# Two-block network on one core: experts on eight chunks of 64 rows instead of four of 128, high and low parts side by side in one stationary operand

## The chip, the cores and the metric

The kernel runs on one core of one Trainium2 chip, in one launch. The metric is the device time of one execution in microseconds, and the time given is the median over several runs. PE is TensorE (matmul), DVE is VectorE, ACT is ScalarE, POOL is GpSimd; SP is the engine that issues the DMAs here.

## The reference, cut to what matters

The network is two layers of a first block, then one second block, on 256 tokens of width 1024. The change is in the last stage, a mixture of 32 experts. A router takes each token to one of four groups, then to two of the eight experts of this group, and gives two weights; every expert is a gated network of width 256:

```python
g_top, g_idx = lax.top_k(g_prob, 1)
e_top, e_loc = lax.top_k(jax.nn.softmax(e_in, axis=-1), 2)
gate = sum(one_hot(e_glob, 32) * weights)
hdn = silu(xc @ w1[e]) * (xc @ w3[e])
out = sum over e of ((hdn * gate[:, e]) @ w2[e])
```

So there are 512 (token, expert) rows. With the reference's own inputs its router picks 20 of the 32 experts. Their rows, in the order of the experts, are 21, 10, 38, 58, 17, 3, 26, 19, 3, 1, 2, 1, 3, 14, 73, 3, 2, 145, 27, 46.

Laid end to end, these 512 rows fall into chunks. With four chunks of 128 the experts in each are 5, 11, 4 and 3 (an expert that crosses a border counts in both chunks). With eight chunks of 64 they are 3, 3, 4, 8, 4, 1, 2 and 2; an expert that ends exactly on a border is counted in the next chunk too. The sixth small chunk lies wholly inside the expert of 145 rows.

## The kernel before, in words

Matrices are kept as two fp32r parts, a high one (the value rounded) and a low one (the rest). A product takes three matmuls: high by high, high by low, low by high (`mm3`, lines 330 to 335). Each matmul has a 128x128 stationary operand and 512 moving columns in this stage.

The stage is `moe`. Weights lie in HBM as units of 128x1024 fp32 (512 KB). An expert has six: q0 to q3 hold w1 and w3, q4 and q5 hold w2. A unit is fetched by SP (`fetch`, line 1729) into one of six `raw` buffers or one of four `held` buffers, then parted by `parts`: ACT writes the high part (line 1743), DVE subtracts it to get the low part (line 1744). `ahead` holds parts of q0 and q1 of the expert to come, `kept` parts of q4 and q5 of a chunk's last expert.

Rows of the tokens are gathered by expert, 128 to a chunk, with matmuls against a placement matrix `P` (`gather`, lines 1810 to 1822) into `xs`, high and low apart. Which experts a chunk has is known only on the chip: DVE makes the lists `table`, `last` and the counts `items` (lines 1779 to 1829), and the engines read them into registers (lines 1756 and 2008).

The loop over the chunks (lines 1997 to 2018) is, for each chunk:

- SP fetches four units of the chunk's end ahead of time into `held`.
- A nest of `If(n > j + 1)`, one level for each further expert of the chunk (line 2011). Each level that is taken runs one `item` (line 1942): 24 matmuls into `g` (`gu`), 12 matmuls `down` for the expert before it, a `turn` of the hidden rows (two transposes on PE, then a split by ACT and DVE), and the fetch and parting of the next units. A chunk with n experts runs n - 2 items. Where a level isn't taken, every engine jumps to the end of the nest.
- The `edge` (line 1954): the last expert of this chunk and, with the same weights, its rows in the next chunk (`g2`). It parts the four held units, two `kept` and two `ahead`, multiplies for both chunks, does two `down`, and then `finish` (line 1888): DVE scales `y` by `g2`, ACT and DVE split it, and eight matmuls with the transposed placement `PT` add it to the 256 token rows in `acc`.

The first expert (`first`, line 1928) runs beside the gather. PSUM holds `acc` (four banks), `y` (two), and one bank each for `gu` and `tr`. Within an engine the order is that of the scheduler; `issue_after` and `after` bind some instructions behind others, such as the parting of the held units behind the split of the `turn` (lines 1959 and 1960).

Of the kernel before, what the change touches and what calls it, by code (L numbers as in the profile page):

```python
# [224 lines left out]
class K:  # L225
# [1425 lines left out]
    def moe(self, xT, rows, late, h):  # L1651
# [14 lines left out]
        self.fold, ef, lo, one_f, S = cut(72, 36), cut(32, 32), cut(64, 4), cut(128, 32), cut(64, 32)  # L1666
        cut = self.cuts(self.wl_p.tile([128, UNIT], F32R, name="wl"))
        before, ones, er, C, M, C2, act, before2, hot = (
            cut(p, n) for p, n in ((128, 128), (128, 128), (32, 32), (128, 66), (128, 128), (128, 128), (64, 4), (32, 64), (64, 136)))
        C, M, C2 = (a.rearrange("p (t e) -> p t e", t=2) for a in (C, M, C2))  # L1670
        hot = hot.rearrange("p (c j) -> p c j", c=4)
        zeros = mo.tile([128, 128], F32R, name="zeros")
        nc.gpsimd.iota(ef, pattern=[[0, 32]], base=0, channel_multiplier=1, allow_small_or_imprecise_dtypes=True)
        nc.gpsimd.iota(lo, pattern=[[128, 4]], base=-1, channel_multiplier=0, allow_small_or_imprecise_dtypes=True)
# [40 lines left out]
        h = self.t1("h")  # L1715
# [39 lines left out]
        def entry(tile, i):  # L1755
# [5 lines left out]
        st, end, t1, t2, act2 = S[:, 0:1], S[:, 1:2], S[:, 4:8], S[:, 8:12], S[:, 12:16]  # L1761
        nc.vector.tensor_copy(st, pe[:, 2:3])
        nc.vector.tensor_add(end, st, pe[:, :1])
        nc.vector.tensor_scalar(t1, lo, 129.0, end, op0=OP.add, op1=OP.min)
# [4 lines left out]
        self.warm(2, mm(rank[:64, :4], before2, act[:32], start=True, stop=True), *idle)  # L1769
        key = S[:, 16:20]  # L1770
        nc.vector.scalar_tensor_tensor(key, act.bitcast(F32), 64.0, rank[:64, :4], op0=OP.mult, op1=OP.subtract)
        nc.vector.tensor_tensor(out=hot[:, :, :32], in0=key.unsqueeze(2).to_broadcast([64, 4, 32]),
                                in1=self.down[:64, None, :].to_broadcast([64, 4, 32]), op=OP.is_equal)
        pl = self.bank("gu")[:32, :132]
        mm(pl[:, :128].rearrange("p (c j) -> p c j", c=4), er, hot[:32, :, :32], start=True, stop=True)
        self.warm(7, mm(pl[:, 128:], ones[:32, :32], act[:32], start=True, stop=True), *idle)
# [3 lines left out]
        lists, count = pl[:1, :128].rearrange("p (c j) -> p c j", c=4), pl[:1, 128:]  # L1780
        tmp = self.t1("list")
        R, n4 = tmp[:1, :136].rearrange("p (c j) -> p c j", c=4), tmp[:1, 136:140]
        six = self.t1("six")[:1, :128].rearrange("p (c j) -> p c j", c=4)
        nc.vector.tensor_scalar_mul(six, lists, 6.0)
        nc.vector.tensor_copy(items[:, :4], count)
        nc.vector.tensor_reduce(R[:, :, 33], six, axis=AX.X, op=OP.max)
        nc.vector.tensor_copy(n4, count)
        few = lambda a: a.to_broadcast([1, 4, 32])
        nc.vector.tensor_tensor(out=R[:, :, :32], in0=iota[:1, None, :32].to_broadcast([1, 4, 32]),
                                in1=few(n4.unsqueeze(2)), op=OP.is_equal)  # L1790
        nc.vector.tensor_tensor(out=R[:, :, :32], in0=R[:, :, :32], in1=few(R[:, :, 33:]), op=OP.mult)
        nc.vector.tensor_tensor(out=R[:, :, :32], in0=R[:, :, :32], in1=six, op=OP.add)
        table = mo.tile([1, 4, 32], I32, name="table")
# [16 lines left out]
        def gather(xs, s, per, bank):  # L1810

            n = s.stop - s.start
            for k in range(0, 8, per):
                for i in range(2):
                    p = bank()[:, :per * n].rearrange("p (d r) -> p d r", d=per)
                    for d in range(per):
                        for t in range(2):
                            mm(p[:, d], rows[t][i][:, 128 * (k + d):128 * (k + d) + 128], P[:, t, s], start=t == 0, stop=t == 1)
                    if i == 0:
                        yield nc.scalar.activation(xs[i][:, k:k + per], p, AF.Copy)  # L1820
                    else:
                        yield nc.vector.tensor_copy(xs[i][:, k:k + per], p)

        last = mo.tile([1, 8], I32, name="last")
# [4 lines left out]
        nc.vector.tensor_copy(last.rearrange("p (c j) -> p c j", c=4), R[:, :, 32:])  # L1829
        x0, x1 = ([mo.tile([128, 8, 256], F32R, name="xs%d%d" % (n, i)) for i in range(2)] for n in range(2))  # L1830
        chunks = [[x[:, :, 128 * c:128 * c + 128] for x in xs] for xs in (x0, x1) for c in range(2)]
# [4 lines left out]
        gate = mo.tile([128, 136], F32, name="gate")  # L1836
        PT = mo.tile([128, 4, 256], F32R, name="PT")

        def gates():


            self.after(nc.vector.tensor_scalar(t1, lo[:64], 129.0, end, op0=OP.add, op1=OP.is_le), placed)
            nc.vector.tensor_scalar(t2, lo[:64], 128.0, st, op0=OP.add, op1=OP.is_ge)
            nc.vector.tensor_mul(t1, t1, t2)
            nc.vector.tensor_scalar(t2, key, 64.0, None, op0=OP.is_lt)
            nc.vector.tensor_tensor(out=hot[:, :, 32:], in0=t1.unsqueeze(2).to_broadcast([64, 4, 2]),
                                    in1=t2.unsqueeze(2).to_broadcast([64, 4, 2]), op=OP.mult)
# [9 lines left out]
            mine = self.wh_p.tile([128, UNIT], F32R, name="wh")[:64]  # L1857
            nc.vector.tensor_mul(mine[:, :512], mask, pg)
            yield
            pi = self.bank("tr")[:, :136]  # L1860
            for c in range(4):
                mm(pi[:, 34 * c:34 * c + 34], mine[:, 128 * c:128 * c + 128], hot[:, c], start=True, stop=True)
            nc.vector.tensor_copy(gate, pi)
            yield
            for c in range(0, 4, 2):
                p = self.bank("tr")
                self.transposes(p, [P[:, t, 128 * (c + i):128 * (c + i) + 128].bitcast(F32) for i in range(2) for t in range(2)])
# [12 lines left out]

        def down(w, hT, y):
            for half in range(2):
                s = slice(512 * half, 512 * half + 512)
                for k in range(2):
                    ks = slice(128 * k, 128 * k + 128)
                    self.mm3(y[half], (hT[0][:, ks], hT[1][:, ks]), (w[k][0][:, s], w[k][1][:, s]), False, k == 1, True)

        def finish(c, y):

            for half in range(2):  # L1890
                s = slice(512 * half, 512 * half + 512)
                nc.vector.tensor_mul(yg[:, s], y[half], g2[:, s])
                if c < 3:
                    self.split(*(a[:, s] for a in parts_yg), yg[:, s])
            for t in range(2):
                for half in range(2):
                    pt, s = PT[:, c, 128 * t:128 * t + 128], slice(512 * half, 512 * half + 512)
                    if c == 3:
# [5 lines left out]
        def hidden(h, g, c, j):  # L1904
            sg = self.t1("sg")
            nc.scalar.activation(sg, g[:, :256], AF.Silu)
            nc.vector.scalar_tensor_tensor(h, sg, gate[:, 34 * c + j:34 * c + j + 1], g[:, 256:], op0=OP.mult, op1=OP.mult)

        def gu(g, c, w, ds):

            for d in ds:
                s = slice(512 * (d % 2), 512 * (d % 2) + 512)
                i = self.mm3(g, (chunks[c][0][:, d], chunks[c][1][:, d]), (w[d // 2][0][:, s], w[d // 2][1][:, s]),
                             d == 0, d == 7, True)
# [27 lines left out]
        def item(c, j, e, prev, follow, y):  # L1942
# [4 lines left out]
            hT = then(gu(g, c, w, range(4)), h)  # L1947
# [6 lines left out]
        def edge(c, e, follow, y):  # L1954
# [6 lines left out]
            if c < 3:  # L1961
# [7 lines left out]
            h2 = self.t1("h2")  # L1969
# [3 lines left out]
            if c == 3:  # L1973
                down(kept, turn(h2), y)
                finish(3, y)
# [21 lines left out]
        for c in range(4):  # L1997
            y = [ps.tile([128, 512], F32, name="y", tag="y", bufs=2) for _ in range(2)]
            for half in range(2):
                if c:  # L2000
                    nc.vector.memset(y[half], 0.0)
                else:
                    mm(y[half], zeros, x0[0][:, :2].rearrange("p a b -> p (a b)"), start=True, stop=True)
# [12 lines left out]
            if c < 3:  # L2016
# [109 lines left out]
```

## Time and profile before

| what | value |
|---|---|
| median of three runs | 1815.82 us (1813.64 to 1819.9) |
| the profiled execution's own time | 1809.89 us |
| its span, first to last instruction | 1808.1 us |
| mean granted TensorE clock | 0.987 |
| PE, DVE, ACT, POOL busy in the span | 1724.7, 1184.7, 936.7, 62.3 us |
| the expert stage from the first item to the last matmul | 1582.5 to 1797.3 us of the span |

The profile is of one execution; busy times are sums over instructions, and a matmul's end is modelled, so the distance from one matmul's start to the next is the better price. "Idle before" names who ended a wait. Times in views are microseconds from the start of the span.

### The profile page before, as it was taken

What the parts mean: (1) busy time and instruction counts of PE and PEld (TensorE: products, weight loads), DVE (VectorE), ACT (ScalarE), POOL (GpSimd) and SP (SyncE); (2) the same over time, 40 slices, a digit from 0 to 9 for tenths busy, and PEclk for the clock granted to TensorE, in tenths of its full rate; (3) what the DMA queues carried; (4) which work ended last, traced back from release to release, by engine and by line L of the source; (5) the groups of instructions that cost most, each with busy time, mean ns of one, the idle gap of its engine ahead of it and who ended that gap; (6) DMA issues with size and microseconds to landing.
All of it is one profiled execution on the core that took longest, in us unless ns stands there. A gap on an engine that the chain in (4) does not pass through costs nothing. (4 is left out here: it accounts for less than half of the span.)

```text
span 1808.1 us, 26098 instructions
## 1 busy us (share of the span) xinstructions
PE 1724.7 (95%) x9663; PEld 1466.7 (81%) x9663; DVE 1184.7 (66%) x1964; ACT 936.7 (52%) x1454; POOL 62.3 (3%) x85
## 2 busy tenths in 40 slices
PE   9999999999999999999999999999999998799997
PEld 7778899899877887778889899877788796577775
DVE  5675785566666556655687466676566568678776
ACT  5444464654544444444366464654444575467653
POOL 0000002000000000000001100000000001000001
PEclk9999999999999999999999999999999998799999
DMA  8866453234677655865554333558655431489872
GB/s 298 299 221 199 153 174 132 94 112 144 220 232 253 196 198 185 286 214 185 186 177 137 112 106 127 173 198 279 227 191 181 153 128 39 164 316 326 300 252 95
DMA packets 105099, 346.17 MB, mean 191 GB/s; under 512 B 12454, under 2 KB 12710, under 8 KB 104808
## 3 DMA queue, kind: packets, MB, share of 16 engines
q1 hardware_dynamic: 104936, 344.14, 56.1%
q8 instruction: 84, 1.38, 0.3%
q14 instruction: 79, 0.65, 0.1%
HBM read 340.95 MB, written 3.15 MB: 190 GB/s over the span
## 5 line engine op out<-in xcount | busy, mean ns | idle before, releaser
L343 DVE TENSOR_TENSOR wl<-raw,wh 128x1024 fp32r<-128x1024 f32 (+2 forms) x356 | 400.6, 1136 | 180.7 <-ACT wh L343 178.4
L343 ACT ACTIVATE wh<-raw 128x1024 fp32r<-128x1024 f32 (+2 forms) x356 | 346.8, 986 | 304.5 <-PE gu L334 150.3
L333 PE MATMUL gu<-wh,xh 128*128 128x512 f32 (+1 forms) x640 | 255.4, 399 | 4.9 <-ACT xh L343 3.7
L335 PE MATMUL gu<-wh,xl 128*128 128x512 f32 (+1 forms) x640 | 248.3, 388 | 1.7 <-DVE xl L343 1.6
L334 PE MATMUL gu<-wl,xh 128*128 128x512 f32 (+1 forms) x640 | 246.5, 385 | 2.5 <-DVE wl L343 2.5
L333 PE MATMUL gu<-xh,wh 128*128 128x256 f32 x832 | 240.7, 289 | 2.3 <-DVE sp L1209 1.9
L334 PE MATMUL gu<-xl,wh 128*128 128x256 f32 x832 | 236.1, 284 | 0.0
L335 PE MATMUL gu<-xh,wl 128*128 128x256 f32 x832 | 235.9, 284 | 0.0
L333 PEld LDWEIGHTS gu<-xh,wh 128*128 128x128 f32 x832 | 159.5, 192 | 4.4 <-issue 3.2
L334 PEld LDWEIGHTS gu<-xl,wh 128*128 128x128 f32 x832 | 159.4, 192 | 1.1 <-issue 1.0
L335 PEld LDWEIGHTS gu<-xh,wl 128*128 128x128 f32 x832 | 159.3, 192 | 0.0
L335 PEld LDWEIGHTS gu<-wh,xl 128*128 128x128 f32 x640 | 120.2, 188 | 29.4 <-DVE xl L343 5.4
L333 PEld LDWEIGHTS gu<-wh,xh 128*128 128x128 f32 x640 | 120.3, 188 | 27.5 <-ACT xh L343 5.8
L334 PEld LDWEIGHTS gu<-wl,xh 128*128 128x128 f32 x640 | 120.6, 188 | 25.8 <-DVE wl L343 5.0
L343 DVE TENSOR_TENSOR wg<-raw,wg 128x1024 fp32r<-128x1024 f32 x68 | 83.3, 1225 | 74.8 <-ACT wg L343 74.4
L343 ACT ACTIVATE wg<-raw 128x1024 fp32r<-128x1024 f32 x68 | 72.0, 1059 | 99.9 <-DMA raw<-wpk 99.7
L343 DVE TENSOR_TENSOR bl<-raw,bh 128x1024 fp32r<-128x1024 f32 x46 | 56.4, 1225 | 73.2 <-ACT bh L343 73.1
L343 ACT ACTIVATE bh<-raw 128x1024 fp32r<-128x1024 f32 x46 | 48.8, 1061 | 80.5 <-PE acc L335 44.8
L1744 DVE TENSOR_TENSOR wl<-raw,wh 128x1024 fp32r<-128x1024 f32 x72 | 85.5, 1218 | 5.9 <-ACT wh L1743 5.8
L343 ACT ACTIVATE hh<-tr 128x256 fp32r<-128x256 f32 x108 | 40.7, 377 | 91.0 <-PE tr L354 88.7
L1743 ACT ACTIVATE wh<-raw 128x1024 fp32r<-128x1024 f32 x72 | 74.2, 1055 | 9.9 <-DMA raw<-wpk 9.4
L333 PE MATMUL acc<-bh,hh 128*128 128x512 f32 x176 | 70.3, 400 | 9.3 <-ACT hh L343 9.0
(589 smaller groups left out, 3551.9 us busy)
## 6 DMA issues: line engine op xcount, KB each, us to landing
raw<-wpk SPq DMA_DIRECT2D x549, 512.0 KB, 4.2
ada<-wada SPq DMA_DIRECT2D x96, 256.0 KB, 5.0
held<-wpk SPq DMA_DIRECT2D x16, 512.0 KB, 4.9
bc_g<-ln_g SPq DMA_DIRECT2D x8, 512.0 KB, 4.8
bc_b<-ln_b SPq DMA_DIRECT2D x8, 512.0 KB, 6.8
raw<-wpk SPq DMA_DIRECT2D x6, 384.0 KB, 3.4
c<-c SPq DMA_DIRECT2D x8, 256.0 KB, 5.7
kept<-n SPq DMA_DIRECT2D x8, 256.0 KB, 3.3
```

The source lines that it names most:

```text
L333: nc.tensor.matmul(out, ah, bh, start=start, stop=False, skip_group_check=skip)
L334: nc.tensor.matmul(out, ah, bl, start=False, stop=False, skip_group_check=skip)
L335: return nc.tensor.matmul(out, al, bh, start=False, stop=stop, skip_group_check=skip)
L343: return nc.scalar.activation(hi, src, AF.Copy), nc.vector.tensor_sub(lo, src, hi.bitcast(F32))
L1743: hi = nc.scalar.activation(wh, raw, AF.Copy)
L1744: lo = nc.vector.tensor_sub(wl, raw, wh.bitcast(F32))
```

## The change

Rows are cut into eight chunks of 64. A chunk's stationary operand holds the 64 high rows in its left half and the 64 low rows in its right half, so that two matmuls (against the high and the low weights) make all four products, and the two halves of the output partitions are added afterwards. `gu` has 16 matmuls instead of 24 and `down` 8 instead of 12. The sum is made in `turn`: ACT copies both halves of `g` out of PSUM (`hidden`), four small fp32 matmuls with a stacked identity (`both`) transpose and add, then ACT takes the Silu, DVE the product, and ACT and DVE split it into the two halves of `hs`. `finish` puts both halves into `acc` by `PT`, whose rows are doubled (`P2`, `PT`). The lists are of eight chunks. `yg` has a buffer of its own, `PT` takes a buffer that held two `raw` tiles, and `raw` has five tiles instead of six.

The diff, cut to its core:

```diff
-        for _ in range(2):
-            more = self.gt.tile([128, 2, 1024], F32, name="raw", tag="gate")
-            raw_tiles += [more[:, i] for i in range(2)]
-        yg = raw_tiles.pop()
+        more, PT = (self.gt.tile([128, 2, 1024], dt, name="raw", tag="gate") for dt in (F32, F32R))
+        raw_tiles += [more[:, i] for i in range(2)]
+        yg = mo.tile([128, UNIT], F32, name="yg")
...
-        x0, x1 = ([mo.tile([128, 8, 256], F32R, name="xs%d%d" % (n, i)) for i in range(2)] for n in range(2))
-        chunks = [[x[:, :, 128 * c:128 * c + 128] for x in xs] for xs in (x0, x1) for c in range(2)]
+        x0, x1 = (mo.tile([128, 8, 4, 2, 64], F32R, name="xs%d" % n) for n in range(2))
+        chunks = [xs[:, :, c].rearrange("p d i r -> p d (i r)") for xs in (x0, x1) for c in range(4)]
...
+            P2 = self.new_xT()[0].rearrange("p d t -> p (d t)").rearrange("p (t c i r) -> p t c i r", t=2, c=8, i=2)
+            for t in range(2):
+                nc.scalar.activation(P2[:, t], P[:, t].bitcast(F32).rearrange("p (c r) -> p c r", c=8)[:, :, None]
+                                     .to_broadcast([128, 8, 2, 64]), AF.Copy)
...
-            for c in range(0, 4, 2):
+            for c in range(0, 8, 2):
                 p = self.bank("tr")
...
+        def hidden(h, g, c, j):
+
+            a, b = h
+            nc.scalar.activation(a, g[:, :256], AF.Copy)
+            nc.scalar.activation(b, g[:, 256:], AF.Copy, scale=gate[:, 34 * c + j:34 * c + j + 1])
+
         def turn(h, tag="tr"):
-            p = one(tag)
-            self.transposes(p, [h[:, :128], h[:, 128:]])
-            hh, hl = self.t1("hh", F32R), self.t1("hl", F32R)
-            split.append(self.split(hh, hl, p[:, :256]))
-            return hh, hl
+
+            p = one(tag)[:, :256]
+            for k in range(2):
+                for i, a in enumerate(h):
+                    mm(p[:, 128 * i + 64 * k:128 * i + 64 * k + 64], a[:, 128 * k:128 * k + 128], both, start=True, stop=True)
+            sg, hid, hs = self.t1("sg")[:, :128], self.t1("hid")[:, :128], self.t1("hs", F32R)
+            nc.scalar.activation(sg, p[:, :128], AF.Silu)
+            nc.vector.tensor_mul(hid, sg, p[:, 128:])
+            two = lambda a: a.rearrange("p (k r) -> p k r", k=2)
+            hs = hs.rearrange("p (k i r) -> p k i r", k=2, i=2)
+            split.append(self.split(hs[:, :, 0], hs[:, :, 1], two(hid)))
+            return hs.rearrange("p k i r -> p k (i r)")
...
+        def mm2(out, x, w, start, stop):
+            mm(out, x, w[0], start=start, stop=False, skip_group_check=True)
+            return mm(out, x, w[1], start=False, stop=stop, skip_group_check=True)
...
-                    self.mm3(y[half], (hT[0][:, ks], hT[1][:, ks]), (w[k][0][:, s], w[k][1][:, s]), False, k == 1, True)
+                    mm2(y[half], hT[:, k], [a[:, s] for a in w[k]], False, k == 1)
...
-            hT = then(gu(g, c, w, range(4)), h)
+            hT = then(gu(g, c, w, range(3)), h)
+            gu(g, c, w, (3,))
...
-        for c in range(4):
+        for c in range(8):
```

## Rows read from the trace of the kernel before

**Rows 1.** Windows, three stretches: PE, PEld, DVE, ACT, POOL busy, clock, DMA share, GB/s

```profile
1629.00:1706.30 77.30, 77.30 (x344) 62.31 (x343) 67.30 (x71) 57.44 (x70) 0.00 (x0) 1.00 0.88 325
...
1779.00:1797.00 18.00, 16.37 (x62) 11.04 (x62) 11.44 (x16) 6.72 (x9) 0.19 (x1) 1.00 0.18 61
...
1620.00:1630.00 10.00, 9.94 (x44) 7.56 (x43) 7.88 (x13) 3.82 (x7) 0.00 (x0) 1.00 1.02 398
```

**Rows 2.** Timeline of PE: the starts of the four edges, waits in brackets

```profile
1610.34 0.47 PE L333 MATMUL gu<-wh,xs 128*128 128x512 f32 x1 [1.97 <-DVEq L2009]
1610.65 0.40 PE L334 MATMUL gu<-wl,xs 128*128 128x512 f32 x1
1610.88 0.40 PE L335 MATMUL gu<-wh,xs 128*128 128x512 f32 x1
...
1708.52 0.47 PE L333 MATMUL gu<-wh,xs 128*128 128x512 f32 x1 [2.00 <-DVEq L2009]
...
1710.36 0.63 PE L333 MATMUL gu<-wh,xs 128*128 128x512 f32 x1
1710.79 0.63 PE L334 MATMUL gu<-wl,xs 128*128 128x512 f32 x1
...
1748.77 0.47 PE L333 MATMUL gu<-wh,xs 128*128 128x512 f32 x1 [1.94 <-DVEq L2009]
...
1779.28 0.47 PE L333 MATMUL gu<-wh,xs 128*128 128x512 f32 x1 [0.77 <-DVEq L2009]
```

**Rows 3.** Timeline of DVE through the second edge: start, length, line, what

```profile
1705.37 1.22 DVE L1744 TENSOR_TENSOR wl<-raw,wh 128x1024 fp32r<-128x1024 f32 x1
1712.78 0.42 DVE L343 TENSOR_TENSOR hl<-tr,hh 128x256 fp32r<-128x256 f32 x1 [6.19 <-ACT hh L343]
1713.72 2.36 DVE L1744 TENSOR_TENSOR wl<-held,wh 128x1024 fp32r<-128x1024 f32 x2 [0.52 <-ACT wh L1743]
...
1720.54 0.47 DVE L1907 SCALAR_TENSOR_TENSOR h<-sg,gate,gu 128x256 f32<-128x256 f32 x1
...
1723.20 0.42 DVE L343 TENSOR_TENSOR hl<-gu,hh 128x256 fp32r<-128x256 f32 x1
1725.22 0.69 DVE L1892 TENSOR_TENSOR raw<-y,g 128x512 f32<-128x512 f32 x1 [1.59 <-PE y L335]
...
1728.94 0.69 DVE L343 TENSOR_TENSOR parts<-raw,parts 128x512 fp32r<-128x512 f32 x1
```

**Rows 4.** Timeline of DVE: first parted units of the first and third edge

```profile
1613.64 2.36 DVE L1744 TENSOR_TENSOR wl<-held,wh 128x1024 fp32r<-128x1024 f32 x2 [0.52 <-ACT wh L1743]
...
1753.38 2.36 DVE L1744 TENSOR_TENSOR wl<-held,wh 128x1024 fp32r<-128x1024 f32 x2 [0.52 <-ACT wh L1743]
```

**Rows 5.** Groups of the stage, 1582 to 1798: busy, mean ns, idle before

```profile
L1744 DVE TENSOR_TENSOR wl<-raw,wh 128x1024 fp32r<-128x1024 f32 x66 | 78.4, 1219 | 5.9 <-ACT wh L1743 5.8
L1743 ACT ACTIVATE wh<-raw 128x1024 fp32r<-128x1024 f32 x66 | 67.9, 1055 | 4.4 <-DMA raw<-wpk 4.1
...
L1906 ACT ACTIVATE sg<-gu 128x256 f32<-128x256 f32 x19 | 7.3, 386 | 7.0 <-PE gu L335 6.9
```

**Rows 6.** Waits of SP's queue, 1560 to 1800: total, times, longest

```profile
SPq L1729 <- DVEq L2009: 22.2, 4, 9.0
```

**Rows 7.** SP at the opening: DMA issues, and the register loads (first and last start)

```profile
1566.90 1.92 SPq L1729 DMA_DIRECT2D held<-wpk  x4
1577.17 36.21 SPq L1729 DMA_DIRECT2D raw<-wpk  x22
...
L1756 SPq TENSOR_LOAD <-last x8: 262/268/283, 1565.4 to 1575.1; - x8
L1756 SPq TENSOR_LOAD <-table x4: 263/265/285, 1569.4 to 1576.4; - x4
...
L2008 SPq TENSOR_LOAD <-items x4: 266/266/272, 1568.9 to 1575.7; - x4
```

**Rows 8.** DMA issues of the page: KB each, median us to landing

```profile
raw<-wpk SPq DMA_DIRECT2D x549, 512.0 KB, 4.2
```

More of the change, by code (lines that the diff above doesn't have):

```diff
@@ L1774, in moe @@
-        pl = self.bank("gu")[:32, :132]
-        mm(pl[:, :128].rearrange("p (c j) -> p c j", c=4), er, hot[:32, :, :32], start=True, stop=True)
-        self.warm(7, mm(pl[:, 128:], ones[:32, :32], act[:32], start=True, stop=True), *idle)
+        self.warm(2, mm(rank[:64, :8], before2, act[:32], start=True, stop=True), *idle)
+        key = S[:, 24:32]
+        nc.vector.scalar_tensor_tensor(key, act.bitcast(F32), 64.0, rank[:64, :8], op0=OP.mult, op1=OP.subtract)
+        nc.vector.tensor_tensor(out=hot[:, :, :32], in0=key.unsqueeze(2).to_broadcast([64, 8, 32]),
+                                in1=self.down[:64, None, :].to_broadcast([64, 8, 32]), op=OP.is_equal)
@@ L1779, in moe @@
+        pl = self.bank("gu")[:32, :264]
+        mm(pl[:, :256].rearrange("p (c j) -> p c j", c=8), er, hot[:32, :, :32], start=True, stop=True)
+        self.warm(7, mm(pl[:, 256:], ones[:32, :32], act[:32], start=True, stop=True), *idle)
         items = mo.tile([1, 8], I32, name="items")
[L1780 to L1783, printed above, removed]
+        lists, count = pl[:1, :256].rearrange("p (c j) -> p c j", c=8), pl[:1, 256:]
@@ L1784, in moe @@
+        R, n8 = tmp[:, :272].rearrange("p (c j) -> p c j", c=8), tmp[:, 272:]
+        six = self.t1("six")[:1].rearrange("p (c j) -> p c j", c=8)
         nc.vector.tensor_scalar_mul(six, lists, 6.0)
-        nc.vector.tensor_copy(items[:, :4], count)
+        nc.vector.tensor_copy(items, count)
         nc.vector.tensor_reduce(R[:, :, 33], six, axis=AX.X, op=OP.max)
[L1787 to L1790, printed above, removed]
+        nc.vector.tensor_copy(n8, count)
@@ L1835, in moe @@
             early[q] = parts(raw, q, copies[2 * q - 2:2 * q] if q else ())
[L1836 to L1837 removed]
+        gate = mo.tile([128, 272], F32, name="gate")
+        PT = PT.rearrange("p a (c t) -> p (a c) t", t=256)
+        both = mo.tile([128, 64], F32, name="both")
         def gates():
[L1842 to L1843 removed]
+            self.after(nc.vector.tensor_scalar(t1, lo[:64], 65.0, end, op0=OP.add, op1=OP.is_le), placed)
+            nc.vector.tensor_scalar(t2, lo[:64], 64.0, st, op0=OP.add, op1=OP.is_ge)
             nc.vector.tensor_mul(t1, t1, t2)
             nc.vector.tensor_scalar(t2, key, 64.0, None, op0=OP.is_lt)
[L1846 to L1847 removed]
+            nc.vector.tensor_tensor(out=hot[:, :, 32:], in0=t1.unsqueeze(2).to_broadcast([64, 8, 2]),
+                                    in1=t2.unsqueeze(2).to_broadcast([64, 8, 2]), op=OP.mult)
             gx = weights(placed)
@@ L1912, in gu @@
                 s = slice(512 * (d % 2), 512 * (d % 2) + 512)
-                i = self.mm3(g, (chunks[c][0][:, d], chunks[c][1][:, d]), (w[d // 2][0][:, s], w[d // 2][1][:, s]),
-                             d == 0, d == 7, True)
+                i = mm2(g, chunks[c][:, d], [a[:, s] for a in w[d // 2]], d == 0, d == 7)
             return i
@@ L1968, in edge @@
                 down(wd, hT, y)
-            h2 = self.t1("h2")
+            h2 = [self.t1("h2") for _ in range(2)]
             hidden(h2, g, c, 32)
@@ L1972, in edge @@
                 parts(fetch(e, q), q, to=kept[q - 4])
-            if c == 3:
+            if c == 7:
                 down(kept, turn(h2), y)
-                finish(3, y)
+                finish(7, y)
                 return
@@ L1996, in moe @@
         parts_yg = [parts_yg[:, i] for i in range(2)]
-        for c in range(4):
+        for c in range(8):
             y = [ps.tile([128, 512], F32, name="y", tag="y", bufs=2) for _ in range(2)]
@@ L2002, in moe @@
                 else:
-                    mm(y[half], zeros, x0[0][:, :2].rearrange("p a b -> p (a b)"), start=True, stop=True)
+                    mm(y[half], zeros, x0[:, 0].rearrange("p c i r -> p (c i r)"), start=True, stop=True)
             ends = [entry(last, 2 * c + i) for i in range(2)]
```

61 lines of the change are left out of this document (28 added, 33 removed).

## The prediction

> **What bounds the kernel now.** I read the windows by stage first, then the timelines of PE and DVE around the chunk borders, then the groups, and last the waits of the DMA queue. In a run of nine items PE is busy for the whole stretch, 77.30 us of 77.30, so an item costs 77.3 / 9 = 8.59 us [rows 1]: 36 matmuls at 0.23 us from start to start [rows 2], with the turn in between. That is the figure the change lowers. Yet DVE is busy for 67.30 us of the same stretch, and the best 10 us of the stage moved 398 GB/s [rows 1], so an expert's six units (3.15 MB) can't come in less than 3.15 / 0.398 = 7.9 us. Matmul, parting and transfer all lie between 7.4 and 8.6 us.
>
> At an edge the bound is another. Take the second edge, from 1708.52 [rows 2]. DVE starts its last operation before it at 1705.37, has nothing to do until the turn at 1712.78, starts on the held units at 1713.72, runs through eight units and two small operations until 1723.62, waits 1.59 us for `y` and starts the last operation of `finish` at 1728.94 [rows 3]. So of an edge of about 21 us DVE's own chain fills all but 1.6. And PE starts an edge only when DVE has passed the jump over the levels not taken: all four waits before an edge end with DVE's sequencer at line 2009 [rows 2], and SP waits for the same, 22.2 us in four times [rows 6].
>
> **The change part by part.** The row counts give 3 - 2, 3 - 2, 4 - 2, 8 - 2, 4 - 2, 0, 0 and 0 items for eight chunks: 12 items where there were 15, and eight edges where there were four. The sixth chunk has one expert, whose units are fetched and multiplied once more with a gate of zero. Units parted: six for the first expert, six for the first chunk's item, eight for each of seven edges and six for the last, four for each of the four items that follow an edge (they use `kept`), six for each of the other seven: 132, where there were 120.
>
> *Item.* PE: 24 matmuls at 0.23 and four small ones, about 0.5 us together (an estimate; at most four times 0.23), 6.0 us. DVE: six units at 1.136 us (the eight of the edge took 1723.20 - 1713.72 less 0.39 for the one operation between [rows 3]) and two operations of 128 columns at about 0.28 (a 256-column one took 0.42, a 512-column one 0.69 [rows 3]): 7.4 us. ACT: six units at 1.06, two copies out of PSUM at 0.39 [rows 5], two smaller operations: under 7.8. So PE is no longer last. An item that follows an edge needs four units, 4.5 + 0.6 = 5.1 us of DVE, less 0.2 that it overlaps, 4.9. A second one costs 7.4, as its units were fetched under the edge. In a run, transfer sets 7.9 and the five `raw` buffers may set more. If the 8.59 of now were wholly the six buffers' turn-round, five would make it 10.3; if they cost nothing, 7.4 stands. I take 8.2, nearest to the transfer's row, for the four later items of the fourth chunk, with 7.4 and 9.6 as the ends of the range.
>
> *Edge.* From the start of PE to the first held unit on DVE it was 3.30, 5.20 and 4.61 us in the three edges [rows 2 to 4], 4.4 on average. After: four matmuls instead of six ahead of the turn, minus 0.5; two more small matmuls, plus 0.3; Silu, product and split where a split was, plus 0.6. That makes 4.8. Then eight units, 9.1. The second turn, 0.6. A wait for `y`: 0 to 1.6 [rows 3], I take 0.3, as PE has 24 matmuls less. `finish` to the start of its last operation, 1728.94 - 1725.22 = 3.7 [rows 3], less 0.4 for the operation of line 1907 that goes: 3.3. The jump, from the start of DVE's last operation to PE's start, 1708.52 - 1705.37 = 3.15 [rows 2, 3]. Sum: 4.8 + 9.1 + 0.6 + 0.3 + 3.3 + 3.15 = 21.2 us from one edge to the next where no item lies between. PE needs only 56 matmuls in it, 12.9 us, all beside DVE. The halved matmuls thus buy about 1 us an edge. The last edge keeps its 18.0 [rows 1]: fewer matmuls, the same chain.
>
> Here a rule of the Trainium skill speaks against the change. The page Trainium Kernel Development and Optimization, Best Practices, says "TensorE tiling speeds up compute but not PSUM evacuation". By it alone four more chunks would cost their two reads of `y` at 0.69, 5.5 us in all; by the rows it is the whole chain of DVE that comes again.
>
> *Opening.* SP loads 16 registers, 0.57 us apart, before its first `raw` fetch at 1577.17 [rows 7]. With eight chunks there are 32: plus 9.1. The lists on DVE double, 13 operations by about 0.13: plus 1.8. So that fetch starts at 1588.1, the sixth lands 4.2 us [rows 8] and five times 1.32 later, at 1598.9, its low part starts at 1600.0, and the first edge at 1603.1, against 1610.34 with three items ahead of it [rows 2]. The doubled placement (two copies of 1024 columns on ACT at 1.06, two more groups of transposes with a copy) costs at most 5 us, and lies beside SP's loads; without that cover the 5 us would show. If the loads aren't all put ahead, the edge starts up to 9.1 us sooner.
>
> *Sum.* From edge to edge: one item 21.2 + 4.9 = 26.1; two 33.5; six 33.5 + 4 x 8.2 = 66.3; two 33.5; three times none 63.6; the last edge 18.0. That is 241.0 us from 1603.1, so the last matmul ends at 1844.1. It ended at 1797.3 (1779.28 and 18.0). The stage is **46.8 us longer**; what follows it is not touched. The profiled execution took 1809.89 us, which gives 1856.7; the median of the runs shown lies 5.9 above it, so I say 1863.
>
> **The rivals.** *Matmul stays the bound (the other side).* In favour: PE's 77.30 of 77.30 [rows 1]. Then an edge costs 12.9 + 1.0 + a gap of 2.0 = 15.9, an item 6.0, the last edge 18.0 less 16 matmuls, 14.3, and SP's loads don't delay the first edge (1594.0). The intervals 21.9, 27.9, 51.9, 27.9, 47.7 and 14.3 end at 1785.6: 1804 us. It decides if an edge without items takes under some 16 us and an item under 6.5. Against: DVE's eight units and `finish` alone are 12.8 us in each edge, after a start of at least 3, and 6.0 us for an item asks for 524 GB/s. Chance 0.04.
>
> *The clock falls in the edges.* After the gap of 2.00 us at 1708.52 the matmuls started 0.43 us apart at 1710.36 to 1710.79, which is 512 columns at 1.2 GHz; after 1.97 us at 1610.34 they stayed at 0.23 [rows 2]. With 24 matmuls less in each edge, PE idles more. If a whole edge ran at the lower level, 56 x 0.43 + 1 + 2 = 27.1 us would pass DVE's 21.2: 5.9 more in seven edges and about 8 in the last, 1912 us. The skill's page TensorE: Matmul & The Clock Gate, Why this matters for your kernels, says to leave no idle gaps between bursts of matmuls since the clock falls; the rows agree for two of four gaps. Chance 0.07.
>
> **How the numbers follow.** Forecast 0.86, clock 0.07, matmul 0.04, 0.03 for a sum near zero. Low end: loads spread (-9.1), all starts at 3.7 (-8.8), no wait for `y` (-2.4), items at 7.4 (-3.2): 1839. High end: starts at 5.6 (+6.4), `y` late by 1.6 (+10.4), items at 9.6 (+5.6): 1886. Beyond lies less than 0.2. A measurement of this kernel tells about 0.3% from no change. Faster 0.04, same 0.03, slower 0.93.
>
> **What would show it.** Right: PE idle time in the edges, ended by DVE's line 1744; an edge interval of 20 to 23 us for chunks six to eight; 132 units parted; SP's first `raw` fetch near 1588; DVE busy about 25 us more. Wrong: PE busy throughout the edges with DVE waiting for `y`; edges well under 18 us; DVE parting held units during the jump.

## The result, and the profile after

The changed kernel takes 1926.7 us (1917.6 to 1927.8), beside 1816.3 for the kernel before in runs on the same chip: 110 us more, a ratio of 1.058 [1.056, 1.061]. The sign was forecast; the time, 1863 with 1839 to 1886 as its range, was not: the miss is 64 us. The profiled execution took 1927.8 us, its span is 1926.0; that is 118 us more than the profiled execution of the kernel before. The layers ahead of the stage account for 6.9 us of it: DVE's operation of line 1677, the last that both kernels share, starts at 1546.99 instead of 1540.09. The code up to there is the same, and in the other runs below, of either kernel, it starts between 1541 and 1553, so this is scatter between executions. From there to the last matmul it is 368 us instead of 257: the stage is 111 us longer, where the sum said 47.

Windows of the changed kernel, to be read beside [rows 1]. The columns are the same. They are cut near the starts of the edges. The first holds the edge of the third chunk and the six items of the fourth; the second the edge of the fifth chunk, which has two items ahead of it; the third and the fourth the edges of the sixth and seventh chunk, which have none; the last is the last edge:

```profile
1688.90:1776.00 87.10, 66.67 (x262) 47.05 (x262) 56.47 (x64) 50.97 (x76) 0.00 (x0) 0.90 0.74 254
1820.00:1841.70 21.70, 16.10 (x70) 11.54 (x70) 13.80 (x18) 11.20 (x18) 0.00 (x0) 1.00 0.57 197
1841.70:1866.20 24.50, 18.81 (x72) 14.28 (x72) 13.90 (x18) 11.29 (x18) 0.00 (x0) 0.85 0.52 175
1866.20:1892.00 25.80, 20.23 (x72) 15.28 (x72) 13.98 (x18) 11.29 (x18) 0.00 (x0) 0.76 0.51 166
1892.00:1915.20 23.20, 19.04 (x59) 12.99 (x59) 11.77 (x17) 7.60 (x12) 0.52 (x1) 0.76 0.13 47
```

Where a run of items had PE busy for all of its 77.30 us, DVE for 67.30 and 325 GB/s, now no engine is busy throughout: PE 77% with the granted clock at 0.90, DVE 65%, ACT 59%, 254 GB/s. That is not an engine at its limit but a chain that goes round through several. The edges are of one kind of work, yet the granted clock is 1.00 in the one with items ahead of it and 0.85 and 0.76 in the two without; the time of each edge is in the second table below.

The chain is in the timeline of that run, one turn of the loop (ACT, DVE and PE; the matmuls of `gu` are left out):

```profile
1718.32 1.00 PE L1890 MATMUL tr<-both,h 128*128 128x64 f32 x8
...
1719.35 0.28 ACT L1892 ACTIVATE sg<-tr 128x128 f32<-128x128 f32 x1 [3.56 <-PE tr L1890]
...
1719.66 0.29 DVE L1893 TENSOR_TENSOR hid<-sg,tr 128x128 f32<-128x128 f32 x1 [4.31 <-ACT sg L1892]
1720.61 2.36 DVE L1743 TENSOR_TENSOR wl<-raw,wh 128x1024 fp32r<-128x1024 f32 x2 [0.66 <-ACT wh L1742]
...
1722.88 2.35 DVE L1743 TENSOR_TENSOR bl<-raw,bh 128x1024 fp32r<-128x1024 f32 x2
...
1725.15 0.28 DVE L343 TENSOR_TENSOR hs<-hid,hs 128x128 fp32r<-128x128 f32 x1
...
1725.59 0.76 PE L1901 MATMUL y<-bh,hs 128*128 128x512 f32 x1 [0.68 <-DVE hs L343]
...
1728.71 0.59 PE L1902 MATMUL y<-bl,hs 128*128 128x512 f32 x1
...
1730.53 1.00 PE L1890 MATMUL tr<-both,h 128*128 128x64 f32 x8
```

The turn at 1718.32 feeds the Silu (`sg`), that the product (`hid`). Both stand at the head of ACT's and DVE's queues, in front of four units still to be parted: both engines wait, 3.56 and 4.31 us, with that work behind them (`wl<-raw` stands for q2 and q3, `bl<-raw` for q4 and q5). Then come q2 and q3, then q4 and q5, then the low part of `hs`, the hidden rows that `down` multiplies; only then can PE start `down` at 1725.59, then six matmuls of `gu`, then the next turn at 1730.53. One lap is 12.2 us here; the next, with `down` at the full clock, takes 10.6. The Trainium skill's page TensorE: Matmul & The Clock Gate (Part 1, Engine queue depths) says that ACT and DVE are strict FIFO; the two waits of 3.56 and 4.31 us, with parting work behind them, agree.

The waits of the stage, 1560 to 1925 (what waited, for what: total us, times, longest), say how often:

```profile
DVE hid L1893 <- ACT sg L1892: 99.8, 21, 9.3
ACT sg L1892 <- PE tr L1890: 94.2, 19, 9.6
...
PE y L1901 <- DVE hs L343: 15.3, 15, 1.6
```

The kernel before had an operation behind the turn too: ACT's half of the split, and DVE's behind that. But in an item one of the four units stood behind it on ACT and none on DVE; the others were parted ahead of it. In its run of nine items (1629.0 to 1706.3) the waits were short. First three lines of the kernel before (`bl`, `bh` is the unit left behind the split), then those of the changed kernel in its six items (1700.0 to 1773.8):

```profile
ACT hh L343 <- PE tr L354: 11.2, 8, 2.5
DVE bl L1744 <- ACT bh L1743: 7.5, 8, 2.3
...
DVE hl L343 <- ACT hh L343: 1.0, 1, 1.0
```

```profile
ACT sg L1892 <- PE tr L1890: 22.1, 6, 5.1
DVE hid L1893 <- ACT sg L1892: 18.0, 6, 4.3
```

Per item that is 1.2 us on ACT and 0.9 on DVE before, 3.7 and 3.0 after.

The timeline of DVE around two edges, the fifth (two items ahead of it) and the sixth (none), answers to [rows 3]:

```profile
1816.18 2.36 DVE L1743 TENSOR_TENSOR wl<-raw,wh 128x1024 fp32r<-128x1024 f32 x2 [1.62 <-ACT wh L1742]
1823.41 0.29 DVE L1893 TENSOR_TENSOR hid<-sg,tr 128x128 f32<-128x128 f32 x1 [4.87 <-ACT sg L1892]
...
1825.02 2.36 DVE L1743 TENSOR_TENSOR wl<-held,wh 128x1024 fp32r<-128x1024 f32 x2 [0.66 <-ACT wh L1742]
...
1838.12 0.69 DVE L343 TENSOR_TENSOR parts<-yg,parts 128x512 fp32r<-128x512 f32 x1
1847.99 0.29 DVE L1893 TENSOR_TENSOR hid<-sg,tr 128x128 f32<-128x128 f32 x1 [9.17 <-ACT sg L1892]
...
1849.60 2.36 DVE L1743 TENSOR_TENSOR wl<-held,wh 128x1024 fp32r<-128x1024 f32 x2 [0.66 <-ACT wh L1742]
```

From the first held unit to the last operation of `finish` it is 1838.12 - 1825.02 = 13.1 us, as in the sum (9.1 + 0.6 + 0.3 + 3.3 = 13.3). From DVE's last operation to the first held unit the sum has 3.15 + 4.8 = 7.95: it is 1825.02 - 1817.3 = 7.7 behind items (1816.18 is the first of two), but 11.5 behind an edge without any. PE says why:

```profile
1838.14 0.50 PE L1924 MATMUL acc<-parts,raw 128*128 128x512 f32 x1 [0.53 <-ACT parts L343]
1842.67 0.77 PE L1924 MATMUL acc<-parts,raw 128*128 128x512 f32 x1 [4.02 <-PEq L2026]
1843.23 0.63 PE L1901 MATMUL gu<-wh,xs 128*128 128x512 f32 x1
...
1845.79 1.80 PE L1890 MATMUL tr<-both,h 128*128 128x64 f32 x8
```

PE waits 4.02 us for its own jump over the nest, it comes back at 1.2 GHz (512 columns in 0.43 from start to start), still has matmuls of the last `finish` to do (`acc<-parts,raw`; the `raw` in it is `PT`, which took that buffer), and the turn takes 1.80 us instead of 1.00.

### The profile page after: what moved, and what is told of

Read it like the earlier page. It is cut to its first block, busy times and chain, and to the rows that moved or that the text cites. A ratio compares the mean times of both kernels' runs of the same rounds, so it can differ in the third digit from the quotient of the medians.

```text
span 1926.0 us, 26536 instructions
## 1 busy us (share of the span) xinstructions
PE 1776.3 (92%) x9729; PEld 1490.4 (77%) x9729; DVE 1211.8 (63%) x2011; ACT 972.1 (50%) x1545; POOL 62.2 (3%) x85
## 3 DMA queue, kind: packets, MB, share of 16 engines
q8 instruction: 93, 1.52, 0.3%
HBM read 347.24 MB, written 3.15 MB: 182 GB/s over the span
## 5 line engine op out<-in xcount | busy, mean ns | idle before, releaser
L334 PEld LDWEIGHTS gu<-wl,xh 128*128 128x128 f32 x640 | 121.2, 189 | 26.1 <-DVE wl L343 5.1
L1901 PE MATMUL gu<-wh,xs 128*128 128x512 f32 x168 | 79.5, 473 | 13.7 <-ACT wh L1742 11.8
L1743 DVE TENSOR_TENSOR wl<-raw,wh 128x1024 fp32r<-128x1024 f32 x68 | 80.9, 1219 | 16.1 <-ACT wh L1742 16.1
L1902 PE MATMUL gu<-wl,xs 128*128 128x512 f32 x168 | 80.1, 477 | 11.3 <-DVE wl L1743 9.8
```

The source lines that it names most:

```text
L334: nc.tensor.matmul(out, ah, bl, start=False, stop=False, skip_group_check=skip)
L1743: lo = nc.vector.tensor_sub(wl, raw, wh.bitcast(F32))
L1901: mm(out, x, w[0], start=start, stop=False, skip_group_check=True)
L1902: return mm(out, x, w[1], start=False, stop=stop, skip_group_check=True)
```

## The experiments

Theory A: the packed turn makes each item a serial loop through PE, ACT and DVE, set by the order in the queues. Rivals: B, TensorE's lower clock makes items and edges long; C, five `raw` buffers; D, the number of chunks alone. All ratios are to the kernel before. The second table has the time from one chunk's `finish` (end of its second operation of line 1914) to the next one's, for the second to the eighth chunk, which run 1, 2, 6, 2, 0, 0 and 0 items. It is of one profiled execution each: the three edges without items together take 69.9 to 75.8 us in the seven runs that leave their code and the nest as it is in the changed kernel, so differences of about 2 us in one of them say little. The last `finish` has no split, so the last column ends about 1 us sooner than the two before it.

| kernel | median, us | ratio to before |
|---|---|---|
| changed | 1926.7 | 1.0584 [1.0562, 1.0606] |
| turn behind q3 | 1909.9 | 1.0494 [1.0477, 1.0512] |
| turn early | 1916.3 | 1.0540 [1.0522, 1.0558] |
| four raw | 1933.3 | 1.0639 [1.0614, 1.0664] |
| loads spread | 1926.1 | 1.0585 [1.0567, 1.0602] |
| split ahead of q4, q5 | 1909.5 | 1.0505 [1.0471, 1.0538] |
| three products | 1909.8 | 1.0502 [1.0468, 1.0536] |
| held first | 1920.8 | 1.0556 [1.0505, 1.0608] |
| before, held first | 1815.8 | 0.9990 [0.9971, 1.0009] |
| combined | 1898.5 | 1.0455 [1.0423, 1.0487] |
| filled | 1902.3 | 1.0468 [1.0436, 1.0501] |
| seven levels | 1914.1 | 1.0536 [1.0496, 1.0575] |
| before, short nest | 1819.0 | 1.0008 [0.9993, 1.0024] |
| all edits | 1888.2 | 1.0370 [1.0334, 1.0406] |

| items in the chunk | 1 | 2 | 6 | 2 | 0 | 0 | 0 |
|---|---|---|---|---|---|---|---|
| forecast | 26.1 | 33.5 | 66.3 | 33.5 | 21.2 | 21.2 | 21.2 |
| changed | 31.9 | 42.0 | 89.2 | 42.8 | 24.7 | 25.6 | 24.5 |
| turn behind q3 | 31.1 | 41.5 | 84.6 | 37.7 | 24.1 | 23.9 | 22.9 |
| turn early | 30.0 | 41.9 | 82.6 | 42.5 | 26.0 | 23.7 | 26.1 |
| four raw | 31.1 | 41.8 | 96.3 | 43.3 | 23.9 | 23.8 | 22.2 |
| loads spread | 31.2 | 41.7 | 88.5 | 43.6 | 25.8 | 23.6 | 23.4 |
| split ahead of q4, q5 | 35.3 | 39.0 | 76.7 | 41.4 | 23.4 | 23.9 | 24.5 |
| three products | 29.3 | 41.2 | 75.7 | 41.4 | 25.7 | 29.0 | 25.1 |
| held first | 30.3 | 41.8 | 87.3 | 44.5 | 22.6 | 23.2 | 21.9 |
| combined | 34.6 | 37.6 | 75.6 | 38.8 | 23.1 | 23.3 | 22.3 |
| filled | 29.8 | 39.0 | 77.8 | 40.5 | 24.4 | 24.1 | 23.5 |
| seven levels | 29.1 | 41.8 | 86.0 | 40.7 | 24.2 | 24.2 | 23.2 |
| all edits | 28.3 | 35.3 | 73.4 | 38.5 | 23.6 | 25.3 | 21.9 |

### Turn behind q3

```diff
...
+            late = list(parted)
...
+            ops = nc.scalar.activation(sg, p[:, :128], AF.Silu), nc.vector.tensor_mul(hid, sg, p[:, 128:])
+            for ins, other in zip(ops, behind):
+                self.after(ins, other)
...
-            hT = then(gu(g, c, w, range(3)), h)
+            hT = then(gu(g, c, w, range(3)), h, "tr", late)
```

> Edit: in an item, the Silu is ordered behind the high part of q3 on ACT and the product behind the low part of q3 on DVE, so that neither engine waits for the turn with parting still to do. Theory A (serial loop: turn, Silu, product, four units parted, low part of hs, down, six matmuls, next turn, because ACT and DVE stand in order behind the Silu and the product): an item falls from 10.4 to 11.6 us to 8.0 to 8.8, the largest sum of an engine or the transfer; 11 items give 20 to 35 us, so 1892 to 1907 us. Rival B (TensorE at 1.2 GHz in the items is the cause): PE has the same work and the same gaps in front of down, items stay above 10 us, within 6 us of 1927. Rival C (five raw buffers instead of six): the same units in the same buffers, within 6 us of 1927.

16.9 us less, 2.9 above theory A's range; the rivals had no gain. (`late` are the two parting operations of q3.) With the order freed, the scheduler put the product behind q5 and the low part of `hs` behind the first unit of the next expert, and PE now waits for `hs`:

```profile
1731.60 0.79 PE L1901 MATMUL y<-bh,hs 128*128 128x512 f32 x1 [3.30 <-DVE hs L343]
1732.19 0.63 PE L1902 MATMUL y<-bl,hs 128*128 128x512 f32 x1
...
1743.16 0.50 PE L1901 MATMUL y<-bh,hs 128*128 128x512 f32 x1 [3.30 <-DVE hs L343]
```

The same gap, 3.29 or 3.30 us, comes eight times in the stage, six of them with `down` at 1.2 GHz behind it, two (one at 1743.16) at the full clock. The loop was opened at one place and closed at another; A and B are not yet apart.

### Turn early

```diff
-            hT = then(gu(g, c, w, range(3)), h)
-            gu(g, c, w, (3,))
+            hT = then(gu(g, c, w, range(1)), h)
+            gu(g, c, w, range(1, 4))
```

> Edit: in an item the turn stands behind two matmuls of the next expert instead of six, nothing else moves. Theory A: four matmuls leave the loop, 0.92 us at 2.4 GHz, 1.7 at 1.2; 11 items give 10 us (7 to 19), so about 1917 us. Rival B: PE does the same work, within 3 us of 1927, or slower if PE waits more. Rival C: within 3 us of 1927.

10.4 us less, as A has it: PE does the same work, only four matmuls leave the loop. In the six long items it is 89.2 - 82.6 = 6.6, or 1.1 an item, in the size that A gives; the chunks with one and two items moved by 0.1 to 1.9.

### Four raw

```diff
-        raw_tiles = [self.raw_p.tile([128, UNIT], F32, name="raw") for _ in range(3)]
+        raw_tiles = [self.raw_p.tile([128, UNIT], F32, name="raw") for _ in range(2)]
```

> Edit: four raw tiles instead of five. Rival C (an item is the turn-round of the raw buffers, so six units through n buffers): an item grows by a quarter, 2.7 us, 11 items give about +30 us, 1957 us. Theory A: DVE and ACT free a buffer in time in any case while they wait for the turn; an item changes by under 0.7 us, the total within 8 us of 1927. Rival B: as A.

6.5 us more, most of it in the six items (96.3 for 89.2, 1.2 each, where C asked for 2.7 and A for under 0.7). C falls as the main cause; a sixth buffer was not tried.

### Loads spread

```diff
+            with tc.issue_after(self.got.ins) if c else ExitStack():
+                ends = [entry(last, 2 * c + i) for i in range(2)]
...
+                n, foll = nc.values_load(items[:1, c:c + 1], min_val=1, max_val=32), c < 7 and entry(flat, 32 * c + 33)
```

> Edit: SP's register loads of the second and later chunks stand behind the last fetch of the chunk before, so 6 instead of 32 stand ahead of the first item's first raw fetch after the opening. If the loads cost what the prediction says (0.57 us each ahead of that fetch): the fetch comes some 13 us earlier, the first item starts 5 to 9 us earlier (then held by the gather and the first expert), and the total falls by 5 to 9 us, to 1918 to 1922. If the opening is bound by the gather, the lists or the placement: within 2 us of 1927. The items and edges don't change in either case; a loss would mean that the spread loads now delay the fetches at the edges.

No change, although SP's fetch moved from 1588.85 to 1581.16 (9.7 us, counted from line 1677). First the changed kernel, then this run (SP's issues, then the first item on PE):

```profile
1588.85 3.08 SPq L1728 DMA_DIRECT2D raw<-wpk  x5
...
1595.82 0.64 PE L1901 MATMUL gu<-wh,xs 128*128 128x512 f32 x1 [0.68 <-DMA raw<-wpk]
```

```profile
1581.16 24.43 SPq L1728 DMA_DIRECT2D raw<-wpk  x6
...
1597.52 0.73 PE L2020 MATMUL y<-xs,zeros 128*128 128x512 f32 x2 [0.69 <-ACT raw L1874]
1598.89 0.49 PE L1901 MATMUL gu<-wh,xs 128*128 128x512 f32 x1 [0.64 <-PE y L2020]
```

Line 1874 is the copy of the transposed, doubled placement (into `PT`, hence the name `raw`). The prediction had it hidden beside SP's loads, and it is as long as they are: in the changed kernel PE waits for it too (0.69 us, to 1594.42), and then 0.68 for the fetch. Taking away one of two that end together gives nothing.

### Split ahead of q4 and q5

The order of the first run, and:

```diff
+            wd = kept if c and j == 1 else [load(prev, q, split[-1]) for q in (4, 5)]
```

> Edit: as the run with the turn behind q3, and the parting of q4 and q5 ordered behind the split, so that the low part of hs is no longer behind three or four units. Theory A in its sharper form (what counts is the way from the turn to down, and from down to the next turn; the run before took it off the waits for the turn, but put hs behind the first unit of the next expert, and PE waited up to 3.3 us for hs): the loop is Silu, product, split (1.3 us), q4 and q5 (2.4 to 3.2), down (1.9), six matmuls (1.4), turn (1.0), about 8 to 9 us at 2.4 GHz, where the long items took 10.0 to 12.9. Total 1885 to 1902 us. If the clock or the transfer sets the long items, they stay above 10 us and the total within 8 us of the run before, 1902 to 1918.

The total is that of the first run, 7 us above the range and inside that of the rivals, but the six items fall from 89.2 to 76.7 us, 2.1 each. The buffers are the same five. The clock alone could not give 12.5 us: at 0.90 over 87.1 us a fifth of the time, 17.4 us, ran at half, so even a full clock throughout would have saved at most 8.7 (an estimate from the window above), and here it is at 0.95. In exchange the chunk with one item took 3.4 us more (see the filled run). ACT now waits for `raw` in the window below too (1.58 us once), at 278 GB/s; whether the transfer has become a limit is not shown (columns as in the windows above):

```profile
1705.00:1775.00 70.00, 58.31 (x246) 41.59 (x247) 51.01 (x56) 48.84 (x70) 0.00 (x0) 0.95 0.81 278
```

### Three products

```diff
-            mm(out, x, w[0], start=start, stop=False, skip_group_check=True)
-            return mm(out, x, w[1], start=False, stop=stop, skip_group_check=True)
+            return self.mm3(out[:64], (x[:, :64], x[:, 64:]), w, start, stop, True)
...
+            [nc.tensor.transpose(p[:, 128 * k:128 * k + 64], h[0][:64, 128 * k:128 * k + 128], self.ident[:64, :64]) for k in range(2)]
```

Silu and product come before the turn again, as in the kernel before.

> Edit: eight chunks as in the changed kernel, but three matmuls per product on 64 rows, with the hidden rows, the turn and the split of the kernel before; the packing alone is undone. Theory A (the packed turn put Silu and product between PE and DVE and made the item a serial loop): although PE gets 50% more matmuls, an item goes back to 8.6 to 9.0 us, PE's own time as in the kernel before, 2 us less in each of 11 items, and edges fall to 21 to 24; total 1880 to 1905 us. Rival D (the number of chunks is the whole cause and the packing does gain): 12 matmuls more in each item and 24 in each edge show, 20 to 50 us more, 1945 to 1975 us. Rival B (clock): as A, since PE has fewer gaps, and then the granted clock must be near 1.0 in the items.

16.9 us less than with two products: 50% more matmuls in `gu` and `down`, and faster. That is 4.8 above A's range, whose edges of 21 to 24 us came out at 25.1 to 29.0, and far under D's. A run of items is PE's again, at the full clock:

```profile
1710.00:1780.00 70.00, 66.89 (x289) 37.37 (x288) 54.01 (x61) 44.74 (x56) 0.00 (x0) 1.00 0.82 296
```

It also splits the loss: eight chunks with the old arithmetic, but still with five `raw` tiles and the doubled placement, cost 5.0% (91 us of 1816), the packing adds 0.8% (15 us). The packing does pay at one place, the three edges without items (79.8 us with three products, 74.8 with two), and loses 13.5 in the six items. So D is right on the larger part, and wrong that the packing gains.

### Held first, in both kernels

```diff
-            hT = then(gu(g, c, ahead, range(2)), h)
-            i = gu(g, c, ahead, range(2, 4))
-            w = ahead + [parts(held[q - 2], q, split[-1]) for q in (2, 3)]
+            i = gu(g, c, ahead, range(2))
+            w = ahead + [parts(held[q - 2], q) for q in (2, 3)]
+            hT, i = then(i, h, "tr", list(parted)), gu(g, c, ahead, range(2, 4))
```

> Edit: in each edge the held units q2 and q3 are parted ahead of the turn's operations instead of behind its split; q4 and q5 stay behind the split. If the prediction's term for the start of an edge (4.8 us in which DVE has nothing to do until the turn) lies on the chain that sets the edge: each edge falls by 2 to 3.5 us, eight give 16 to 28, 1899 to 1911 us. If PE's own path (matmuls at the lower clock, then hs and down) bounds the edge: within 5 us of 1927.

> The same edit on the kernel of four chunks: in its four edges q2 and q3 are parted ahead of the turn's split. If DVE's chain with its idle start bounds its edges too: 1 to 2.4 us in each, 4 to 10 in all, 1806 to 1813 us beside about 1816. If PE bounds them (21.1 of 21.2 us busy): within 3 us of the kernel before.

In the edges without items, DVE starts its chain 5.67 us behind its last operation instead of 11.0 to 11.5, but the three edges together take 67.7 us, where the same edge code took 69.9 to 75.8: 0.7 to 2.7 us each:

```profile
1840.99 0.69 DVE L343 TENSOR_TENSOR parts<-yg,parts 128x512 fp32r<-128x512 f32 x1
1846.66 2.36 DVE L1743 TENSOR_TENSOR wl<-held,wh 128x1024 fp32r<-128x1024 f32 x2 [4.98 <-ACT wh L1742]
1849.90 0.29 DVE L1892 TENSOR_TENSOR hid<-sg,tr 128x128 f32<-128x128 f32 x1 [0.88 <-ACT sg L1892]
...
1860.24 0.69 DVE L1914 TENSOR_TENSOR yg<-y,g 128x512 f32<-128x512 f32 x1 [1.31 <-PE y L1902]
```

Part of what was gained at the start is given back to the turn (0.88 here, 1.52 and 2.03 in the next two) and to `y` (1.31): PE's path lies close behind DVE's. The total, 6 us less, lies between the two forecasts, and the intervals overlap. With four chunks nothing is gained that shows: there PE is busy throughout the edge, as the window in the next section shows.

### Combined, filled, seven levels, and all of them

Combined: the orders of the split ahead of q4 and q5, the turn behind two matmuls, the held units first.

> Edit: three earlier edits together: in an item the turn's operations behind q3 with q4 and q5 behind the split, the turn behind two matmuls of the next expert instead of six, and in an edge the held q2 and q3 ahead of the turn's operations. If the serial loop of the items and the idle start of the edges are separate terms, as theory A and the edge's sum say, the gains add: 17 for the items, 5 to 10 for the earlier turn (less than the 10 measured alone, as the loop is shorter now), 6 to 18 for the edges; 1882 to 1900 us. If one clock or one transfer limit stands behind all of them, the total stays at 1905 or above.

28 us less than the changed kernel, inside the range. By the ratios the parts are 0.8, 0.4 and 0.3%, together 1.5; the combination has 1.3. Within the intervals they add, as separate terms would; the third part alone is not clear of noise.

Filled, on the run with the split ahead of q4 and q5:

```diff
+                for _ in range(6): i = mm(y[0], zeros, x0[:, 0].rearrange("p c i r -> p (c i r)"), start=False, stop=False, skip_group_check=True)
```

> Edit: on the run with the split ahead of the down units, six matmuls against zeros are put in front of down in each item, 1.4 us more for PE at 2.4 GHz, in the time in which it waits for hs or the last part. Rival B (TensorE at 1.2 GHz makes the remaining length of the items): the gap in front of down is filled, the clock stays up, an item loses 1 to 2 us, 1890 to 1900 us. Theory A (the order of the parts on ACT and DVE sets the loop, PE only waits in it): between 4 us less and 8 us more than that run, 1905 to 1918, as the filler takes the place of the wait.

72 matmuls more, 7 us less by the medians, between the two forecasts, and the intervals overlap. From 1610 to 1700 us the granted clock is 0.97 where it was 0.87 without them. The gain is in the chunk with one item, 29.8 us for 35.3: its clock was 0.85 in the run without the zeros (1630 to 1665) and is 1.00 here (1627 to 1657), and the 3.4 us that this chunk had lost are back. The same chunk falls from 34.6 in the combined run to 28.3 with all edits, its clock from 0.80 to 1.00. The six long items did not gain (77.8 for 76.7). So B has a share, and by these runs the smaller one.

Seven levels:

```diff
-                for j in range(1, 31):
+                for j in range(1, 8):
```

> Edit: the nest of conditional items of the changed kernel has 7 levels instead of 30, so the jump over levels not taken is a quarter as far in the code (a chunk of more than nine experts isn't computed; with these inputs no chunk has more than eight). If the price of a jump grows with its distance or with the levels passed: DVE's 3.1 us and PE's 4.0 us shrink by 1 to 2 us in each of eight chunks, 8 to 16 us in all, 1911 to 1919. If any taken jump of this kind costs the same: within 3 us of 1927.

12.6 us less by the medians (the intervals overlap a little). The group of line 2026 on DVE's queue (compares of the nest, and the first semaphore behind a jump; the last two numbers are the first and last start), in the changed kernel and then here, and the wait of PE here:

```profile
L2026 DVEq COMPARE_BRANCH  x24: 43/52/67, 1609.9 to 1888.9; - x24
...
L2026 DVEq EVENT_SEMAPHORE  x8: 21/21/21, 1612.8 to 1891.9; - x8
```

```profile
L2026 DVEq COMPARE_BRANCH  x24: 43/47/67, 1609.1 to 1876.4; - x24
...
L2026 DVEq EVENT_SEMAPHORE  x8: 21/21/21, 1610.5 to 1876.9; - x8
```

```profile
PE acc L1924 <- PEq L2026: 13.1, 7, 4.0
```

The first jump falls from 2.9 to 1.4 us, the last from 3.0 to 0.5. But PE still waits up to 4.0 us for its own jump, and the three edges without items take 71.7 us, within the 69.9 to 75.8 of the long nest. The Trainium skill's page Runtime: NRT & Kernel Launch (Instruction fetch mechanics) says that a taken branch to a target outside the pages at hand forces a fetch before execution goes on. That DVE's jump falls from 2.9 to 1.4 and from 3.0 to 0.5 us over the shorter nest agrees; that a fetch is what it waits for, and why PE's stays, is not shown.

Before, short nest (the same edit with eleven levels on four chunks):

> Edit: the kernel of four chunks with 11 levels of conditional items instead of 30 (a chunk of more than thirteen experts isn't computed; with these inputs no chunk has more than eleven). In the eight chunks seven levels took DVE's jump from 2.8 to 3.1 us down to 1.3 to 1.4 where items came before it. If that price is on the chain of the edges here too (all four PE waits ahead of an edge end with DVE's jump): 1 to 2 us in each of four edges, 4 to 8 us in all, 1808 to 1812 beside about 1816. If PE's own length bounds the edge: within 2 us of the kernel before.

No gain. DVE's jumps fell (the last from 2.8 to 1.0 us), and PE's own took their place: 1.9 us at the longest, where all four waits of [rows 2] were for DVE.

```profile
PE gu L333 <- PEq L2009: 4.2, 3, 1.9
...
PE gu L333 <- DVEq L2009: 0.5, 1, 0.5
```

> Edit: the combined run, the filler of six matmuls in front of down in each item, and seven levels instead of 30 (a chunk of more than nine experts isn't computed). If loop, start of the edge, clock in the items and jump are separate terms: 1898 less 7 for the filler and 8 to 13 for the jumps, 1878 to 1885 us, still 60 or more above four chunks, because eight edges remain. If the jump's gain was the clock's or the loop's under another name: 1890 or above.

38.6 us less than the changed kernel, a little above the range. By the ratios 1.3% (combined), 0.4 (filler) and 0.5 (levels) make 2.1, which is what came. Even so eight chunks stay 3.7% above four. No version here beats the kernel before.

## Why the prediction was wrong

**The sign and, for the changed kernel, the mechanism of the edge were right.** The chain from the first held unit to the last operation of `finish` was put at 13.3 us and took 13.1; PE idles in the edges; 132 units are parted; DVE is busy for 1211.8 us on the page, 27 more than before, where 25 was said. Four more edges are four more laps of that chain. Neither rival came whole: matmul did not stay the bound (PE at 77% in the items), and no edge ran at 1.2 GHz throughout, though 0.76 and 0.85 are part of the way. For the kernel before the reading was wrong: PE, not DVE's chain, fills its second edge, 21.12 of 21.20 us, and two edits on that kernel that shorten DVE's way gained nothing.

```profile
1708.50:1729.70 21.20, 21.12 (x85) 16.48 (x86) 14.30 (x18) 11.07 (x15) 0.00 (x0) 0.92 0.92 327
```

**The step that failed is the item.** It was priced as the largest of three sums that run side by side: 4.9 behind an edge, 7.4 for the second, 8.2 for later ones. The four chunks with items exceed the forecast by 5.8, 8.5, 22.9 and 9.3, 46.5 us for eleven items, 4.2 each. The step that fails is the overlap: the change puts two operations that wait for PE in front of all four units that ACT and DVE part in an item. The prediction asked of every engine how long it works, not what stands behind the instruction that waits. The old product came before the turn, and the old split, which did wait for it, had at most one unit behind it; the new product comes behind the turn. The sums were nearer: less the run's own edges without items (24.9 on average), one of the six items takes 10.7 us, where the forecast has 7.5 on average. With the order freed it is 8.8 in the run with the split ahead of q4 and q5 and in the combined one, 8.3 with all edits, and 8.2 with three products. So about two of the three microseconds are the loop. What holds the rest is open: the run of nine items moved 325 GB/s over its length and the freed runs here less, and the 398 from which 8.2 was taken stands for 10 us only.

**The start of an edge without items** was mis-sized by 3.0 to 3.5 us: taken from edges that had items ahead, where the sum held (7.7 for 7.95). Three such chunks exceed by 3.5, 4.4 and 3.3, 11.2 in all. Part of it is the clock, which the prediction had as a rival with 5.9 an edge: PE came back at 1.2 GHz behind gaps of 3.6 to 4.0 us.

**The opening and the last edge**: Counted as the sum counts, from the first matmul of `gu` in one edge to the next edge's, the intervals are 31.9, 45.0, 87.9, 43.0, 23.8, 24.2 and 25.9 us, and the last edge, said to keep its 18.0, takes 21.8. The four with items exceed the sum by 48.4, the three without by 10.3, the last edge by 3.8; the first edge starts at 1611.59, 1.6 later than the sum less the 6.9 of the earlier layers. These make the 64. (The three without were to be 20 to 23.) SP's first fetch at 1588.85 for 1588.1 is luck: 6.9 of it is the earlier layers, so it came 4.8 us later than in the kernel before, where 10.9 was said, because 23 registers were loaded ahead of it and not 32. The first edge depends little on it: the run with spread loads moved the fetch by 9.7 us and gained nothing, as the placement's copies end at the same time.

## What to carry to other kernels

When a change moves an operation from one side of a cross-engine hop to the other, list what stands behind it in the in-order queue: an engine that is 65% busy can still set the time if its work waits behind a result of another engine. Saving matmuls in a stage where matmul, parting and transfer lie close together bought nothing here, as the chain between them did not get shorter too. And a finer tiling that repeats a fixed chain (unit loads, parting, jump, `finish`) is priced by the chain, not by the rows saved: 5.0 of the 5.8% here.

## What the runs showed of the hardware

The price of a jump over levels not taken was not fixed: on DVE 2.8 to 3.1 us over a nest of 30 levels, 0.5 to 1.4 over seven, while PE still waited up to 4.0 for its own over seven. Where zero matmuls were put into a wait, the granted clock of a stretch was 0.97 and not 0.87, and the run was not longer. And the length of a gap on PE alone did not tell the clock behind it: behind 2.26 us it was 1.00 in the edge, behind 4.02, 3.55 and 3.79 it was 0.85, 0.76 and 0.76, but behind 2.04 (to 1776.02) matmuls started 0.43 us apart from 1777.60 on, and two of the eight gaps of 3.3 us in the run with the turn behind q3 were followed by the full clock.
